# All direct tiles of a block ahead of its products, in a kernel for one step of a streaming encoder

## Chip, core and metric

The kernel runs on one core of a Trainium2 chip. The metric is the device time of one launch in microseconds. A core has five engines with their own instruction streams: TensorE (PE; its weight loads are listed as PEld), VectorE (DVE), ScalarE (ACT), GpSimd (POOL) and SyncE (SP), which here issues nearly all DMAs. They wait for each other through semaphores.

## The reference

One layer with post-norms, on 2048 prompt tokens and 128 sample tokens (8 sequences of 16), width 1024. In short:

```python
qm, km, vm, om, ip, fp, qa, ka, va = split_in(x @ w_in)       # 1024 -> 2824
hm = mlstm_chunkwise(qm, km * 128 ** -0.5, vm, ip + b_igate, log_sigmoid(fp + b_fgate), C0, n0, m0, chunk)
hm = sigmoid(om) * head_norm(hm, g_mlstm_norm)
ha = windowed_attention(rope(qa), rope(ka), va, attn_sinks)    # 8 query heads, 2 key heads
h = layer_norm(ALPHA * x + concat([hm, ha]) @ w_out)
a, g = split(causal_conv3(h @ w_up) + b_conv)                  # 1024 -> 2 * 2816
y = layer_norm(ALPHA * h + (silu(g) * a) @ w_down)
```

Both groups of tokens go through it; beside `y` it returns the states of the memory, the last keys and values and the last rows of the convolution. This case concerns the first line, `x @ w_in`. Its columns fall in two parts: 2560 of them (queries, keys, values, output gate) and 264 (four forget gates, four input gates, and the keys and values of the attention, 128 each).

## The kernel before

All matrices are multiplied in fp32r with three matmuls for one: each operand is split into a high part (a cast on ScalarE, L218 or L566) and a low part (the difference, on VectorE, L219 or L567), and high by high, high by low and low by high are added up in PSUM.

**Stages.** First the input projections in four blocks of four prompt tiles of 128 tokens (`IBLOCKS`; the sample tile belongs to block 0), with the mLSTM and attention work woven in as "chains"; then the output projection in five output blocks (`OBLOCKS`), with the rest of the chains; then the ConvFFN. TensorE's order is the order in which the program is written. The other engines' order is chosen by a scheduler that goes by the order of the program and by when it expects operands to be ready; within one engine, and in SyncE's queue, instructions run in that order.

**Products.** The 2560 columns are done in five groups g (0 to 4) per block. Within a group a matrix product of 2 x 2 sub-blocks is done with seven products instead of eight (a Strassen-like scheme); they are the steps s = 1, 7, 6, 2, 5, 4, 3. Each needs one combination of the token quadrants and one of the weight quadrants. An item `("p", b, g, s)` is one such product: 24 matmuls of 256 columns (L705), and in block 0 for four of the steps 12 more for the sample tile (L715). The results collect in three PSUM banks `ib`, and `i_after` evicts them.

**Direct tiles.** The 264 columns are done directly: an item `("t", b, i, e)` multiplies tile i of block b by the gate weights, 24 matmuls of 264 columns (L731, `i_direct`), into bank `ib[0]` or `ib[2]`. `i_keys` evicts them (ScalarE, L739 and L740), applies the rotary embedding (VectorE, L869 to L872) and stores keys and values (SyncE, L742). The gate weights come in four units of 264 KB, loaded and split anew for every e.

**Tokens.** The tokens of a block are four quadrants of 512 KB, `xr` 1 to 4: quadrants 1 and 3 are the first and second half of the features of tiles 0 and 1, quadrants 2 and 4 those of tiles 2 and 3. `x_load` loads them, and `x_steps` makes the combinations: the split quadrants "1", "2" (quadrant 3), "3" (quadrant 4) and "b12" (quadrant 2), and the sums "t3", "t2", "t1", "t4" with the splits 7, 6, 5 and 4. The direct tiles 0 and 1 need the splits 1 and 2, tiles 2 and 3 need "b12" and 3. A split is kept in a slot of its step, which is free for the next block when the last product of that step is done.

**Order before.** Block 0 begins with its direct tiles 2 and 3, then come the first product and the sample's direct tile. Its direct tiles 0 and 1 come at the end of the block, followed by tiles 2 and 3 of block 1, and so on: at each change of block stand tiles 0 and 1 of the old block and 2 and 3 of the new one, and behind the last block its tiles 0 and 1. `passages` lists after which step of the last group each combination for the next block is made; those of quadrants 1 and 3 (steps 1 and 2) are made behind direct tile 1. For the start, `i_dense` writes out the order of loads and splits; the loads are tokens 2, the gate units, tokens 4, the sample tokens, rotary tables, tokens 1, the weights of group 0, and tokens 3.

**Weaving.** `Chains.weave` adds up a planned cost for each bit of dense work (645 for six matmuls) and lets a chain take its next step when its own due time has passed. While a direct tile of block 1 or later is done, `hold` keeps the chains back. `i_done`, which opens the next block to the chains, is set some items behind the end of a block (`after`).

Of the kernel before, what the change touches and what calls it, by code (L numbers as in the profile page):

```python
# [16 lines left out]
KD = D // P  # L17
# [188 lines left out]
class Prog:  # L206
# [131 lines left out]
    def i_begin(self):  # L338
# [3 lines left out]
        for b in range(nb):  # L342
            if b == 0:
                it += [("t", 0, i, -1) for i in (2, 3)]

                it += [("p", 0, 0, 1), ("t", 0, 4, -1), ("p", 0, 0, 2), ("p", 0, 1, 1), ("p", 0, 0, 7), ("p", 0, 0, 6)]
            else:
                it += [("p", b, 0, s) for s in (1, 7, 6, 2)]
            for g in range(NG):
                if b == 0:  # L350

                    it += [("p", b, g, s) for s in (6, 2)] * (g > 0) + [("p", b, g, 5)]
                    if g + 1 < NG:
                        it += [("p", b, g + 1, 1)] * (g > 0) + [("p", b, g, 4), ("p", b, g, 3), ("p", b, g + 1, 7)]
                    else:
                        it += [("p", b, g, 3), ("p", b, g, 4)]
                elif g + 1 < NG:

                    it += [("p", b, g, s) for s in (6, 7, 2)] * (g > 0)
                    it += [("p", b, g, 5), ("p", b, g + 1, 1), ("p", b, g, 3), ("p", b, g, 4)]  # L360
                else:
                    it += [("p", b, g, s) for s in (6, 7, 5, 2, 3, 4)]
            it += [("t", b, i, b) for i in (0, 1)]
            if b + 1 < nb:
                it += [("t", b + 1, i, b) for i in (2, 3)]
# [169 lines left out]
    def x_load(self, b, *qs):  # L535
        for q in qs:
            self.xr[b, q] = r = self.x_raw(q)
            self.nc.sync.dma_start(r, self.a["xq"][b][(q - 1) // 2, (q - 1) % 2])

    def x_steps(self, b, *steps):  # L540
# [3 lines left out]
        for s in steps:  # L544
# [14 lines left out]
            else:  # L559
# [3 lines left out]
                n = 4 if (b, s) == (0, "b12") else 1  # L563
# [24 lines left out]
    def i_dense(self):  # L588
# [5 lines left out]
        self.x_load(0, 2)  # L594
        for _ in range(3):
            self.next_raw()
        self.x_load(0, 4)
# [3 lines left out]
        self.rope_load(IBLOCKS[0][2], 2)  # L601
        self.rope_load(NPT, 1)
        self.next_split()
        self.x_steps(0, "b12")
        for _ in range(3):
            self.next_split()
        self.x_steps(0, 3)
        self.x_single(1, 2)
        self.x_load(0, 1)
        self.next_raw()  # L610
        self.x_load(0, 3)
        self.x_steps(0, 1)
        self.advance()
        self.x_steps(0, 2, "t3", 7, "t2", 6)
# [4 lines left out]
        passages = [{1: ["load"], 7: ["t3", 7], 6: ["t2", 6], 3: [3, "t4"], 4: ["b12", "t1"]},  # L619
                    {1: ["load"], 6: ["t3"], 7: [7, "t2"], 5: [6], 3: [3, "t4"], 4: ["b12", "t1"]}]  # L620
        sums = 0
        after = None
        for item in self.items:
# [9 lines left out]
            if item[0] == "t":  # L633
# [3 lines left out]
                if b not in self.gates:  # L637
                    self.gates[b] = self.tp.tile([P, 5, 8], F32, name="gates", tag="gates", bufs=2)
                ps = self.bank([P, 512], "pg") if ti == 4 else self.ib[ti % 2 * 2]
                yield from self.i_direct(b, ti, e, ps)  # L640
                self.i_keys(b, ti, ps)
                if ti == 1:
                    if b + 1 < nb:
                        self.x_steps(b + 1, 1, 2)
                    else:
                        self.release(4)
                    after = [6, b + 1]
                elif ti == 3 and b or ti == 4:
                    self.release(4)
                    self.x_steps(b, 4)  # L650
                    if b:
                        self.x_steps(b, 5)
# [14 lines left out]
            if (g, s) == (1, 6):  # L667
                self.rope_load(IBLOCKS[b][0], 2)
            if g == last and b + 1 < nb:
                if s == 7:  # L670
                    self.rope_load(IBLOCKS[b + 1][2], 2)
# [47 lines left out]
    def i_direct(self, b, ti, e, ps):  # L719

        mm = self.nc.tensor.matmul
        for k in range(KD):
# [1473 lines left out]
```

## Time and profile before

| | us |
|---|---|
| median of 3 runs | 2306.43 |
| lowest, highest | 2305.89, 2309.27 |
| the profiled execution's own time | 2306.25 |
| its span in the profile | 2304.5 |
| TensorE busy in the span | 2278.9 (99%) |
| VectorE busy | 1807.4 (78%) |
| ScalarE busy | 1272.4 (55%) |

How to read what follows. Views of the profile name work as line, engine, operation, and out<-in by the program's names. In a timeline a row is: start, duration (both us), engine, line, operation, tiles, sizes, count, and in brackets the idle time of the engine ahead of it with what ended that. In a table by stretch a row is: from:to, length, then for PE, PEld, DVE, ACT and POOL the busy time with the number of instructions in brackets, then the granted clock of TensorE (1 is full), the busy share of the DMA engines, and GB/s; where the table is for one line alone, only the engines of that line stand in it. Matmuls overlap, so the time from one start to the next is what counts, not the duration shown.

### The profile page before, as it was taken

How to read it: one execution, taken by the hardware profiler on the slowest of the kernel's cores; microseconds unless marked ns; L12 is line 12 of the kernel's file. 1: busy time of each engine (PE TensorE's matmuls, PEld its weight loads, DVE VectorE, ACT ScalarE, POOL GpSimd, SP SyncE). 2: the span in 40 equal slices, each digit the busy share in tenths (PEclk: the TensorE clock that was granted, in tenths of full speed). 3: DMA queues.
4: the chain of work that ended last, by engine and by line, in shares of the span. 5: the costliest groups of instructions: out<-in, count | busy, mean ns of one | idle time of the engine just before them, and what ended most of it. 6: DMA issues, size and time to landing. Idle time of an engine off the chain costs nothing.

```text
span 2304.5 us, 39741 instructions
## 1 busy us (share of the span) xinstructions
PE 2278.9 (99%) x14293; PEld 2094.4 (91%) x14293; DVE 1807.4 (78%) x3075; ACT 1272.4 (55%) x2377; POOL 279.4 (12%) x509
## 2 busy tenths in 40 slices
PE   8999999999999999999999999999999999999998
PEld 8999999989877778999999999999999978888876
DVE  8787587787688888998778777678766786895987
ACT  5453476776766656555656555556555544444442
POOL 0001001100011210211112101003111200200200
PEclk9999999999999999999999999999999999999999
DMA  7988999899987757888777888878998786746742
GB/s 267 319 306 297 309 322 342 310 306 341 309 286 239 242 199 277 302 328 300 277 281 272 307 304 310 306 256 289 316 299 260 248 299 213 253 170 223 253 156 83
DMA packets 300165, 632.38 MB, mean 274 GB/s; under 512 B 47868, under 2 KB 141120, under 8 KB 299968
## 3 DMA queue, kind: packets, MB, share of 16 engines
q1 hardware_dynamic: 295296, 616.14, 77.3%
q0 software_dynamic: 3520, 10.56, 1.4%
q10 hardware_dynamic: 1152, 3.15, 0.4%
q8 instruction: 113, 1.85, 0.3%
q14 instruction: 84, 0.69, 0.1%
HBM read 458.11 MB, written 171.64 MB: 273 GB/s over the span
## 4 chain that ended last, share of the span: by engine, by line
PE 81%; DVE 4%; DMA 2%; issue 1%; ACT 1%; POOL 0%; SPq 0%; DVEq 0%; ACTq 0%; POOLq 0%
PE dps L1874 19%; PE fup L1874 19%; PE dps L705 8%; PE fup L2081 6%; PE dps L2081 6%; PE fht L2081 6%; PE dps L223 3%; PE dps L224 2%; PE dps L225 2%; PE ppo L1349 1%; PE psc L1304 1%; PE ppt L1343 1%; PE dps L731 1%; PE fht L1698 1%; PE pscore L1129 1%
## 5 line engine op out<-in xcount | busy, mean ns | idle before, releaser
L1874 PE MATMUL fup<-hh,uw 128*128 128x384 f32 (+1 forms) x1848 | 478.4, 328 | 0.0
L1874 PE MATMUL dps<-hh,uw 128*128 128x384 f32 (+1 forms) x1848 | 478.0, 328 | 0.0
L1874 PEld LDWEIGHTS fup<-hh,uw 128*128 128x128 f32 x1848 | 330.5, 188 | 0.0
L1874 PEld LDWEIGHTS dps<-hh,uw 128*128 128x128 f32 x1848 | 330.3, 188 | 0.0
L1932 DVE SCALAR_TENSOR_TENSOR cc<-u,cw,cc 128x768 f32<-128x768 f32 (+1 forms) x264 | 258.2, 979 | 62.8 <-ACT cc L1930 56.1
L1874 PE MATMUL fup<-hl,uw 128*128 128x384 f32 (+1 forms) x924 | 303.2, 328 | 0.9 <-DVE hl L219 0.9
L1874 PE MATMUL dps<-hl,uw 128*128 128x384 f32 (+1 forms) x924 | 302.8, 328 | 0.0
L705 PE MATMUL dps<-w,oh 128*128 128x256 f32 x1344 | 254.2, 284 | 0.0
L218 ACT CAST uw<-wraw 128x1024 fp32r<-128x1024 f32 x126 | 123.3, 979 | 230.4 <-PE dps L2081 122.4
L219 DVE TENSOR_TENSOR w<-wraw,w 128x1024 fp32r<-128x1024 f32 (+2 forms) x167 | 189.7, 1142 | 66.0 <-ACT w L218 61.9
L218 ACT CAST w<-wraw 128x1024 fp32r<-128x1024 f32 (+2 forms) x167 | 163.0, 984 | 119.0 <-PE dps L705 61.9
L705 PEld LDWEIGHTS dps<-w,oh 128*128 128x128 f32 x1344 | 210.7, 188 | 10.8 <-issue 8.1
L219 DVE TENSOR_TENSOR uw<-wraw,uw 128x1024 fp32r<-128x1024 f32 x126 | 142.5, 1131 | 62.3 <-ACT uw L218 62.2
L705 PE MATMUL dps<-w,ol 128*128 128x256 f32 x672 | 188.1, 280 | 0.0
L1874 PEld LDWEIGHTS fup<-hl,uw 128*128 128x128 f32 x924 | 173.9, 188 | 1.7 <-DVE hl L219 1.5
L2081 PE MATMUL fup<-uw,fu 128*128 128x512 f32 x726 | 174.0, 396 | 1.2 <-ACT fht L2089 1.2
L1874 PEld LDWEIGHTS dps<-hl,uw 128*128 128x128 f32 x924 | 173.8, 188 | 0.0
L705 PE MATMUL dps<-oh,w 128*128 128x256 f32 x896 | 169.6, 285 | 3.6 <-DVE w L219 1.3
L2081 PEld LDWEIGHTS fup<-uw,fu 128*128 128x128 f32 x726 | 136.6, 188 | 34.3 <-ACT fht L2089 1.6
L2081 PE MATMUL dps<-uw,fu 128*128 128x512 f32 x660 | 165.3, 396 | 1.1 <-DVE uw L219 1.1
L1930 ACT ACTIVATE cc<-u,cw 128x768 f32<-128x768 f32 (+1 forms) x132 | 132.0, 1001 | 46.2 <-DVE u L1912 22.2
L2081 PEld LDWEIGHTS dps<-uw,fu 128*128 128x128 f32 x660 | 124.1, 188 | 31.2 <-DVE uw L219 1.5
(318 smaller groups left out, 4590.0 us busy)
## 6 DMA issues: line engine op xcount, KB each, us to landing
uw<-zw SPq DMA_DIRECT2D x176, 512.0 KB, 5.1
zw<-uw SPq DMA_DIRECT2D x88, 512.0 KB, 3.3
w<-zws SPq DMA_DIRECT2D x72, 512.0 KB, 5.8
wv<-wup SPq DMA_DIRECT2D x66, 512.0 KB, 4.4
wraw<-wi SPq DMA_DIRECT2D x65, 512.0 KB, 5.5
wraw<-zt SPq DMA_DIRECT2D x60, 512.0 KB, 4.1
wraw<-wdn SPq DMA_DIRECT2D x45, 512.0 KB, 4.5
wraw<-wo SPq DMA_DIRECT2D x40, 512.0 KB, 4.7
```

Of the source, the lines that this page charges most:

```text
L218: nc.scalar.copy(hi, src)
L219: return nc.vector.tensor_sub(lo, src, hi.bitcast(F32)).ins
L223: mm(out, ah, bh, start=start, stop=False)
L224: mm(out, ah, bl, start=False, stop=False)
L225: mm(out, al, bh, start=False, stop=stop)
L705: mm(o, l, r, start=s in (1, 7) and c == k == i == 0, stop=k == 3 and i == 2, skip_group_check=True)
L731: mm(o, x, w, start=k == i == 0, stop=k == KD - 1 and i == 2, skip_group_check=True)
L1129: self.nc.tensor.matmul(ps[:, h], qk[:, 4 + h], qk[:, h], start=True, stop=True)
L1874: mm(ps, l[:, k], r[:, k], start=s in (1, 7) and k == 0 and i == 0, stop=k == 3 and i == 2, skip_group_check=True)
L1930: S.activation(c[:, v], u[:, 2:2 + n], AF.Identity, bias=w[3], scale=w[2])
L1932: V.scalar_tensor_tensor(c[:, v], u[:, i:i + n], w[i], c[:, v], op0=ALU.mult, op1=ALU.add)
L2081: mm(ps, l[:, k, c], r[:, k], start=s in (1, 4, 7) and u == 0 and k == 0 and i == 0, stop=u == nu - 1 and k == n - 1 and i == 2, skip_grou ...
```

## The change

The direct tiles of a block all come ahead of its products: block 0 begins with its tiles 0 to 3, and at a change of block stand the four tiles of the new block. Behind the last block there are none, and the gate weights are loaded for four sets e instead of five. Tiles 0 and 1 of block 0 are done together by halves: the first four of the eight feature blocks for both, into `ib[0]` and `ib[2]`, then the second four for both, then both evictions. At the start quadrant 1 is loaded first and in two DMAs of two feature blocks each, and split in four pieces (before, quadrant 2 was split in four pieces); quadrant 3 is loaded after the second gate unit; the splits follow in the order 1, 2, "b12", 3. For the other blocks the splits 1 and 2 move into the last group, behind its steps 2 and 5 in block 0 and behind step 2 in the later ones. The rotary tables of both pairs of tiles are loaded at one place. The counter `after` starts behind the last product and counts 8 items instead of 6, so that it ends at the same product of the next block.

```diff
@@ i_begin
-                it += [("t", 0, i, -1) for i in (2, 3)]
+                it += [("t", 0, i, -1) for i in (1, 2, 3)]
...
-            it += [("t", b, i, b) for i in (0, 1)]
             if b + 1 < nb:
-                it += [("t", b + 1, i, b) for i in (2, 3)]
+                it += [("t", b + 1, i, b) for i in range(4)]
@@ x_load
-            self.nc.sync.dma_start(r, self.a["xq"][b][(q - 1) // 2, (q - 1) % 2])
+            x = self.a["xq"][b][(q - 1) // 2, (q - 1) % 2]
+            n = 2 if (b, q) == (0, 1) else 1
+            for i in range(n):
+                k = slice(i * 4 // n, (i + 1) * 4 // n)
+                self.nc.sync.dma_start(r[:, k], x[:, k])
@@ x_steps
-                n = 4 if (b, s) == (0, "b12") else 1
+                n = 4 if (b, s) == (0, 1) else 1
@@ i_dense
         self.next_raw()
-        self.x_load(0, 2)
-        for _ in range(3):
+        self.x_load(0, 1)
+        self.next_raw()
+        self.x_load(0, 3)
+        for _ in range(2):
             self.next_raw()
-        self.x_load(0, 4)
+        self.x_load(0, 2, 4)
...
-        self.rope_load(IBLOCKS[0][2], 2)
+        for i in (0, 2):
+            self.rope_load(IBLOCKS[0][i], 2)
         self.rope_load(NPT, 1)
         self.next_split()
-        self.x_steps(0, "b12")
-        for _ in range(3):
+        self.x_steps(0, 1)
+        self.next_split()
+        self.x_steps(0, 2)
+        for _ in range(2):
             self.next_split()
-        self.x_steps(0, 3)
+        self.x_steps(0, "b12", 3)
         self.x_single(1, 2)
-        self.x_load(0, 1)
         self.next_raw()
-        self.x_load(0, 3)
-        self.x_steps(0, 1)
         self.advance()
-        self.x_steps(0, 2, "t3", 7, "t2", 6)
+        self.x_steps(0, "t3", 7, "t2", 6)
...
-        passages = [{1: ["load"], 7: ["t3", 7], 6: ["t2", 6], 3: [3, "t4"], 4: ["b12", "t1"]},
-                    {1: ["load"], 6: ["t3"], 7: [7, "t2"], 5: [6], 3: [3, "t4"], 4: ["b12", "t1"]}]
+        passages = [{1: ["load"], 7: ["t3", 7], 6: ["t2", 6], 2: [1], 5: [2], 3: [3, "t4"], 4: ["b12", "t1"]},
+                    {1: ["load"], 6: ["t3"], 7: [7, "t2"], 5: [6], 2: [1, 2], 3: [3, "t4"], 4: ["b12", "t1"]}]
...
+                if b == 0 and ti == 1:
+                    for h in range(2):
+                        for i in range(2):
+                            yield from self.i_direct(b, i, e, self.ib[i * 2], (h,))
+                    self.i_keys(b, 0, self.ib[0])
+                    self.i_keys(b, 1, self.ib[2])
+                    self.advance()
+                    continue
...
-                if ti == 1:
-                    if b + 1 < nb:
-                        self.x_steps(b + 1, 1, 2)
-                    else:
-                        self.release(4)
-                    after = [6, b + 1]
-                elif ti == 3 and b or ti == 4:
+                if ti == 3 and b or ti == 4:
...
-            if (g, s) == (1, 6):
-                self.rope_load(IBLOCKS[b][0], 2)
+            if (g, s) == (last, 4):
+                after = [8, b + 1]
...
-                    self.rope_load(IBLOCKS[b + 1][2], 2)
+                    for i in (0, 2):
+                        self.rope_load(IBLOCKS[b + 1][i], 2)
@@ i_direct
-    def i_direct(self, b, ti, e, ps):
+    def i_direct(self, b, ti, e, ps, halves=(0, 1)):
...
-        for k in range(KD):
+        for k in [4 * h + i for h in halves for i in range(4)]:
```

## The prediction

> **What bounds the kernel now.** I read the head of the page first, then who TensorE waited for between 100 and 700 us, then the stretches of the start.
>
> ```profile
> span 2304.5 us, 39741 instructions
> PE 2278.9 (99%) x14293; PEld 2094.4 (91%) x14293; DVE 1807.4 (78%) x3075; ACT 1272.4 (55%) x2377; POOL 279.4 (12%) x509
> ...
> PE ppt L1518 <- POOL v L1094: 2.9, 1, 2.9
> PE pnum L1212 <- issue: 1.9, 2, 1.4
> PE dps L705 <- ACT mr L1154: 0.8, 1, 0.8
> PE ppo L1349 <- ACT pth L1344: 0.6, 1, 0.6
> ```
>
> TensorE is busy 99% of the span: 25.6 us are left idle, and a change that moves matmuls without removing any can win only idle time and time at a lower clock. In the second view (waits by engine and line: total, times, longest) no direct tile (L731) stands: the changes of block at 155, 292, 453 and 620 us cost TensorE nothing today, so nothing is to be won there. What is left for this change is the start. The next two views are stretches: of the direct tiles alone, of the products (L705) alone, and of all engines.
>
> ```profile
> 5.99:18.26 12.27, 9.89 (x48) 8.72 (x47) 0.72 1.03 408
> 155.07:166.74 11.67, 11.67 (x96) 11.62 (x96) 1.00 0.93 307
> 620.34:626.28 5.94, 5.94 (x48) 5.89 (x48) 1.00 0.82 290
> ...
> 38.16:45.63 7.47, 5.17 (x28) 4.56 (x26) 0.77 0.85 292
> 45.63:48.52 2.89, 2.89 (x24) 2.86 (x24) 1.00 0.98 398
> ...
> 9.00:12.00 3.00, 1.20 (x3) 0.89 (x4) 2.06 (x3) 2.18 (x3) 0.00 (x0) 0.70 1.04 408
> 12.00:17.00 5.00, 5.00 (x24) 5.00 (x24) 3.76 (x9) 2.78 (x8) 0.00 (x0) 0.50 1.03 421
> 41.00:45.00 4.00, 3.94 (x21) 3.73 (x19) 4.00 (x6) 1.03 (x3) 0.00 (x0) 0.59 0.79 229
> ```
>
> Four direct tiles take 11.67 us when nothing is late (0.122 us a matmul, two tiles 5.84). At the start two tiles take 12.27: 6.4 us are lost there, and the granted clock (the number before the DMA share) is 0.70 and then 0.50 behind the waits. The product of step 6 (38.16 to 45.63) takes 7.47 us where the next takes 2.89: 4.6 us more. These two places are most of what can be had.
>
> ```profile
> 8.01 0.39 PE L731 MATMUL dps<-w,oh 128*128 128x264 f32 x1 [0.46 <-DVE w L219]
> 10.36 0.81 PE L731 MATMUL dps<-w,oh 128*128 128x264 f32 x2 [1.47 <-ACT oh L566]
> 11.62 0.59 PE L731 MATMUL dps<-w,ol 128*128 128x264 f32 x1 [0.45 <-DVE ol L567]
> 26.11 0.39 PE L705 MATMUL dps<-ol,w 128*128 128x256 f32 x1 [0.42 <-DVE ol L567]
> 35.66 0.50 PE L705 MATMUL dps<-oh,w 128*128 128x256 f32 x2 [0.48 <-DVE w L219]
> 39.21 0.38 PE L705 MATMUL dps<-oh,w 128*128 128x256 f32 x1 [0.78 <-ACT w L218]
> 40.55 0.53 PE L705 MATMUL dps<-oh,w 128*128 128x256 f32 x2 [0.84 <-DVE w L219]
> 45.63 0.38 PE L705 MATMUL dps<-oh,w 128*128 128x256 f32 x1 [0.69 <-ACT zev L772]
> ...
> 4.13 0.41 ACT L566 CAST oh<-xr 128x256 fp32r<-128x256 f32 x1 [2.11 <-DMA xr<-xq]
> 9.26 1.04 ACT L566 CAST oh<-xr 128x1024 fp32r<-128x1024 f32 x1 [0.61 <-DMA xr<-xq]
> ...
> 4.56:18.26 13.70, 11.32 (x52) 9.77 (x52) 10.83 (x22) 8.72 (x18) 0.00 (x0) 0.75 1.01 391
> 18.26:40.43 22.17, 19.78 (x160) 18.81 (x158) 21.46 (x29) 12.16 (x17) 0.00 (x0) 1.00 0.58 200
> ```
>
> These are TensorE's and ScalarE's rows in order of time (what was waited for in brackets) and two stretches of all engines. The wait of 1.47 us is for the second quadrant of tokens, which lands at 9.2 us (ScalarE's row). From 26 to 41 us every wait ends with VectorE or with the cast in front of it, and VectorE is busy 21.46 of 22.17 us there. So the start has two limits: DMA until about 10 us, VectorE until 40.5.
>
> **The change, part by part.**
>
> *Matmuls moved.* Tiles 0 and 1 of each block go from behind its products to in front of them: 48 matmuls, 5.84 us, more at the start, and the last block's pair (5.94 us at 620.34) is gone. Sum 0. The four gate-weight units of the last block (264 KB each, a cast and a subtraction each) go too; nothing waited for them, 0.
>
> *Order of loading.* Before: quadrant 2, four gate units, quadrant 4; the first half tile needs 512+528 KB, all 48 matmuls 2080 KB. After: quadrant 1 in two halves, two gate units, quadrant 3, the other units, then 2 and 4. The 2080 KB were in at 9.2 us, the first 512 at 4.1: 307 KB a us (estimate from the two ScalarE rows), later 421 GB/s. In the new order that gives unit 0 at 5.0, unit 1 at 5.8, quadrant 3 at 7.5, the last unit at 9.2, quadrant 2 at 10.5, quadrant 4 at 11.7. The next rows price the work on them (VectorE by form up to 45 us: busy, mean ns; SyncE's issues).
>
> ```profile
> L567 DVE TENSOR_TENSOR ol<-xr,oh 128x1024 fp32r<-128x1024 f32 x5 | 6.1, 1223 | 0.9 <-ACT oh L566 0.9
> L219 DVE TENSOR_TENSOR w<-wraw,w 128x528 fp32r<-128x528 f32 x4 | 2.8, 708 | 0.7 <-ACT w L218 0.6
> L872 DVE TENSOR_TENSOR zev<-zev,rb 128x128 f32<-128x128 f32 x3 | 0.9, 289 | 0.0
> L871 DVE TENSOR_TENSOR zev<-zev,ropet 128x128 f32<-128x128 f32 x3 | 0.9, 288 | 0.0
> L869 DVE TENSOR_TENSOR rb<-zev,ropet 128x64 f32<-128x64 f32 x3 | 0.7, 225 | 1.2 <-ACT zev L739 1.1
> L870 DVE TENSOR_TENSOR rb<-zev,ropet 128x64 f32<-128x64 f32 x3 | 0.7, 219 | 0.0
> ...
> 39.28 3.49 DVE L219 TENSOR_TENSOR w<-wraw,w 128x1024 fp32r<-128x1024 f32 x3
> ...
> 0.74 0.39 SPq L538 DMA_DIRECT2D xr<-xq  x1
> 15.70 8.47 SPq L742 DMA_DIRECT2D zkv<-zev  x2
> 24.70 1.76 SPq L456 DMA_DIRECT2D wraw<-wi  x3
> ```
>
> *TensorE at the start, after.* It starts at 5.99 as now, the warm-up ends there. The first halves of both tiles are 24 matmuls, 2.9 us, with some 0.8 us of waits for the low parts of units 0 and 1 (now 0.46): done at 9.7. The second halves need quadrant 3's low part: 7.5 + 1.04 (cast) + 1.23 = 9.8, then unit 2's: + 0.71 = 10.5. A wait of 0.8 us, where there were 1.47 and 0.45. Done at 13.4. Tiles 2 and 3 follow without a wait (quadrant 4's low part at 11.7 + 2.3 = 14.0, needed at 14.9) and end at 19.2. Now this point is 18.26 with two tiles: 5.84 - 0.94 = 4.9 us won there.
>
> *VectorE then.* It keeps that gain or takes it back. Its work up to the low part of step 6 (the first of three at 39.28, so 40.5) is the same splits and sums, plus the rotary of tiles 0 and 1: 0.289 + 0.288 + 0.225 + 0.219 = 1.02 us each, 2.0 in all. Its idle time up to there is 2.87 + 0.71 = 3.6 us. I take it that 1.3 us of that is filled, as all four quadrants have landed by 11.7 and VectorE has work from 14 us on without a break; the other 2.3 lie ahead of 14 us, where it waits for landings in both orders. So the low part comes at 40.5 + 2.0 - 1.3 = 41.2. Bounds: 2.0 later if nothing is filled, 1.6 earlier if all is. TensorE would reach that product at 19.2 + (38.16 - 18.26) less the waits of 0.42 and 0.48 = 38.2, so VectorE still sets the pace; some waits of the start come back in front of steps 7 and 6, and I let the lower clock there stand. Step 6 ends 0.7 us later than now with 5.84 us more behind it: 5.1 us won, between 3.8 and 7.4. The wait of 0.69 behind it is for the eviction of the same bank and stays.
>
> *Queues.* SyncE issues one load more for the halves and one rotary table more (0.4 us each); its queue runs ahead of the landings, 0. It also stores the keys of four tiles, not two, each behind a rotary: those two stores held it from 15.70 to 24.17 now, and the next group's weights went out at 24.70. Held some 4 us longer they would go out near 29; the group that they belong to has its other products behind the one that starts at 45.63: 0. ScalarE gets two more evictions of keys into its idle time. The direct tiles of the first block share two banks; tile 2 must wait for tile 0's eviction, which has the 1.46 us of tile 1's second half: 0, at worst 0.3.
>
> *Changes of block.* The splits of quadrants 1 and 3 for the next block (two casts of 1.04, two subtractions of 1.22) move from between the direct tiles to the last group, since their slots are free after its steps 1 and 2. They must be done when step 4 ends, two products later (5.7 us). VectorE is full there at the third change:
>
> ```profile
> 445.00:450.00 5.00, 5.00 (x48) 4.73 (x48) 4.72 (x18) 4.46 (x12) 0.59 (x1) 1.00 0.74 248
> 450.00:455.00 5.00, 5.00 (x46) 5.00 (x45) 4.93 (x7) 5.00 (x15) 0.57 (x1) 1.00 0.89 302
> ...
> 285.00:290.00 5.00, 5.00 (x45) 5.00 (x44) 2.75 (x7) 2.53 (x4) 1.29 (x2) 1.00 0.83 259
> ...
> 873.95 0.61 ACT L897 CAST oh<-xraw 128x512 fp32r<-128x512 f32 x1
> ```
>
> 9.65 of 10 us, while ahead of the second change (285 to 290) almost half is free. What waits behind those splits is the next block's quadrants 4 and 2, due two direct tiles (5.84 us) later. I take 0, with -1.5 to +3 as bounds: the gain if the waits of 1.9 and 0.8 us above shrink because VectorE is freer behind the change of block.
>
> *The end of the projections.* The chains of attention and memory pause during direct tiles; the last pair falls away, so they enter the output blocks up to 5.9 us behind in that order. What hangs on them last is the final quarter of tokens for the last output block: its cast is at 873.95 us (last row above), and TensorE, which waits for no such cast now, needs it some microseconds later (not shown how many). I take 0, with 2 as the far end (half the shift not covered; an estimate).
>
> **Sum.** 2306.25 (the profiled execution, 1.75 us outside its span) - 5.1 = 2301.2. That execution is 0.2 us under the median of 2306.43.
>
> [...]
>
> **Rivals.**
> 1. *The clock holds in front of step 6.* It was 0.59 for 21 matmuls in 4 us, 0.19 us each against 2.89/24 = 0.12: 1.5 us. For it: TensorE's matmuls arrive more evenly. Against it: VectorE is as late as now. 2301.2 - 1.5 = 2299.7.
> 2. *VectorE hides the gain.* None of its idle time is filled (3.8 us) and a wait of the kind seen now at 26 us (0.42) and another of 0.8 in front of a bank turn up: 2304. For it: it has 2 us more work ahead of the same deadline.
> 3. *The last group becomes late: slower.* If, at 453 us, the moved splits end behind step 4, TensorE stands at the first direct tile and falls to half clock. Price by the start: a wait of about 2.4 us and 4.0 more for the lower clock (6.4 lost less 2.4), 6.4 a place. One place eats the 5.1; two make 2314. It decides from a delay of about 3 us of that subtraction on. For it: 9.65 of 10 us busy. Against: the splits are spread over two products, and only one of three places is so full.
> 4. *The halves do nothing*, because the loads are issued in another order than written: the start waits as now, VectorE still limits: 2302 to 2303, inside the second rival's range.
>
> **How the numbers follow.** Forecast 0.48 (own range 2299.8 to 2302.8), rival 1 0.14, rivals 2 and 4 together 0.23, rival 3 0.15. The predicted time is the likeliest's. The range 2297.5 to 2307.5 takes in rivals 1 and 2 and the bounds of the changes of block, and leaves out most of rival 3. A change under 0.2% (4.6 us) can hardly be told from none: below 2301.8 lie rival 1 and three quarters of the forecast, 0.51; above 2311.0 most of rival 3, 0.14; the rest 0.35.
>
> **What would show it.** Right: four direct tiles from about 6 to 19 us, no wait over 1 us before 14 us; step 6's low part at about 41; no L731 wait at the three changes of block; since each change of block has four direct tiles as before, these start about 0.7 us later than now (155.07), and the gain shows only where the output blocks start: about 621, not 626.3. Wrong: a clock of 0.5 between 9 and 17 us again; a wait at a first direct tile for a low part (L567); waits in the output blocks, where there is none now.

## The result and the profile after

The changed kernel takes 2312.3 us (median of 18 runs, 2307.65 to 2317.83) against 2307.15 for the kernel before (18 runs, 2303.51 to 2313.78): a ratio of 1.0025, 95% interval 1.0017 to 1.0032. It is slower by 5 to 6 us (4 to 7 by the interval), where a gain to 2301.2 was forecast. The profiled execution took 2312.08 us.

The head of the page after:

```profile
span 2310.3 us, 39709 instructions
PE 2279.2 (99%) x14293; PEld 2093.3 (91%) x14293; DVE 1807.8 (78%) x3071; ACT 1270.5 (55%) x2373; POOL 280.0 (12%) x509
```

Who TensorE waited for in it between 100 and 640 us (total, times, longest):

```profile
PE ppt L1351 <- ACT pth L1352: 4.1, 2, 2.7
PE ppt L1526 <- POOL v L1102: 2.9, 1, 2.9
PE dps L713 <- ACT mr L1162: 2.1, 1, 2.1
PE dps L713 <- ACT zev L772: 2.1, 1, 2.1
PE pnum L1220 <- DVE dt L1141: 2.0, 1, 2.0
```

Before, the list began with 2.9, 1.9, 0.8 and 0.6. The 2.9 for GpSimd is the same wait; five new ones of 1.4 to 2.7 us have come (four rows), all behind ScalarE or VectorE in the work of attention and memory (L1351, L1220) or in the products (L713, which was L705), and none at a direct tile (L739, which was L731). The start and the changes of block, by stretch, in the columns explained above:

```profile
12.00:17.00 5.00, 5.00 (x44) 5.00 (x43) 3.77 (x6) 2.89 (x8) 0.00 (x0) 1.00 1.04 413
41.00:45.00 4.00, 2.92 (x23) 2.72 (x24) 4.00 (x9) 2.19 (x3) 0.00 (x0) 1.00 0.97 316
...
154.41:166.10 11.69, 11.69 (x99) 11.69 (x98) 9.54 (x19) 5.88 (x12) 0.00 (x0) 1.00 0.87 300
292.80:304.50 11.70, 11.70 (x99) 11.70 (x98) 11.34 (x21) 7.41 (x16) 0.00 (x0) 1.00 0.93 308
459.70:471.40 11.70, 11.70 (x99) 11.70 (x98) 11.36 (x23) 9.82 (x23) 0.00 (x0) 1.00 0.85 288
```

The start does more than was forecast: the clock is 1.00 where it was 0.50 (12 to 17 us, which the forecast had counted on) and 0.59 (41 to 45 us, which it had not). At the changes of block TensorE has no gap. So the loss lies between them. TensorE's order is the same in both kernels from block 1 to the end of the projections, so the start of each matmul can be set against the start of the same one before. Where the changed kernel has done two more direct tiles by then, their 5.84 us are taken off. The difference (negative is ahead), worked out from the traces:

| at us of the trace before | 57 | 253 | 262 | 320 | 345 | 410 | 505 | 570 | 900 |
|---|---|---|---|---|---|---|---|---|---|
| after | -6.6 | -6.5 | -4.9 | -5.5 | -1.5 | +0.9 | -0.6 | +5.2 | +5.6 |

6.6 us are won at the start and kept to 253 us. Then, up to 570 us, 11.7 are lost: 1.6 at 254, 4.0 and 2.4 between 320 and 410, 5.8 between 505 and 570, less gains of 0.6 and 1.5 between. Two stretches there, for TensorE alone (busy time with the number of matmuls, granted clock, DMA share, GB/s), first of the kernel before and then of the changed one:

```profile
320.00:345.00 25.00, 23.09 (x187) 1.00 1.01 343
500.00:530.00 30.00, 29.46 (x247) 1.00 0.99 336
```

```profile
320.00:345.00 25.00, 20.77 (x156) 0.93 0.91 307
500.00:530.00 30.00, 27.05 (x204) 0.94 0.88 285
```

31 and 43 matmuls fewer in the same time: waits, and a lower clock behind them. Following one of them back gives the cause. These are VectorE's, ScalarE's and TensorE's rows of the changed kernel in order of time (in brackets the idle time and what ended it):

```profile
323.45 0.69 DVE L859 TENSOR_TENSOR txy<-txy 128x512 f32<-128x512 f32 x1 [2.21 <-DMA txy<-wdn]
324.06 0.15 DVE L1319 SCALAR_TENSOR_TENSOR amx<-amx,nsink 128x4 f32<-128x4 f32 x1
326.95 0.69 DVE L860 TENSOR_TENSOR txy<-txy 128x512 f32<-128x512 f32 x1 [2.74 <-DMA txy<-wdn]
...
324.31 0.41 ACT L1324 ACTIVATE sc<-sc,amx 128x129 f32<-128x129 f32 x1 [4.88 <-DVE amx L1319]
331.77 0.17 ACT L1162 ACTIVATE mr<-pnum 128x2 f32<-128x2 f32 x1 [4.38 <-DVE bst L1159]
...
327.04 0.39 PE L713 MATMUL dps<-oh,w 128*128 128x256 f32 x1 [2.10 <-ACT zev L772]
333.44 0.38 PE L713 MATMUL dps<-oh,w 128*128 128x256 f32 x1 [2.13 <-ACT mr L1162]
```

L859 to L862 are the sums of the down weights. The ConvFFN at the end also works with sums of weight quadrants, and `d_sums` makes them in blocks 2 and 3, ahead of their use: two loads of 512 KB (L853, L854) into a tile `txy`, which lies in the slots of `xr` 1 and 3, four subtractions on VectorE, two stores. Nobody needs them for a long time. But VectorE works in its order. It stands 2.21 and 2.74 us for the loads, and behind it stand the last step of the softmax's maximum (L1319; the maxima it works on were done at 321.24 us, and it runs at 324.06, behind L859), for which ScalarE waits 4.88 us, and the statistics of the norm (L1159), for which it waits 4.38; ScalarE's own evictions (L772) stand behind these, and TensorE waits 2.10 for such an eviction and then 2.13, by its row for L1162, which had itself waited those 4.38. Before, at this place the sums came behind that work and stood for nothing:

```profile
323.51 0.46 DVE L1151 BATCH_NORM_STATS2 bst<-pnum 128x6 f32<-128x128 f32 x2
332.13 0.69 DVE L851 TENSOR_TENSOR txy<-txy 128x512 f32<-128x512 f32 x1
332.85 0.69 DVE L852 TENSOR_TENSOR txy<-txy 128x512 f32<-128x512 f32 x1
```

Over 300 to 570 us VectorE's waits for `txy` are, before and then after (total, times, longest):

```profile
DVE txy L852 <- DMA txy<-wdn: 4.6, 3, 3.6
DVE txy L851 <- DMA zqk<-zev: 4.2, 1, 4.2
DVE txy L851 <- DMA txy<-wdn: 2.9, 1, 2.9
```

```profile
DVE txy L859 <- DMA txy<-wdn: 13.4, 5, 3.5
DVE txy L860 <- DMA txy<-wdn: 5.4, 3, 2.7
```

11.7 us became 18.8. (One row of before, 4.2, is put down to another DMA than the load.) The sum of these waits is not the price: it grew by 7.1 and TensorE lost 11.7, while two other kernels below (the start alone, and the kernel before without the logs) have waits of 12.0 and 12.9 and TensorE loses 0.2 us or less over the same stretch. What counts is what stands behind each. A load takes 5.5 us from issue to landing before and 6.4 after (medians of the DMA view over the same stretch, 512 KB each):

```profile
txy<-wdn SPq DMA_DIRECT2D x15, 512.0 KB, 5.5
```

```profile
txy<-wdn SPq DMA_DIRECT2D x16, 512.0 KB, 6.4
```

### The profile page after: what moved, and what is told of

Its sections match the earlier page's. It is cut to its first block, busy times and chain, and to the rows that moved or that the text cites. A ratio compares the mean times of both kernels' runs of the same rounds, so it can differ in the third digit from the quotient of the medians.

```text
span 2310.3 us, 39709 instructions
## 1 busy us (share of the span) xinstructions
PE 2279.2 (99%) x14293; PEld 2093.3 (91%) x14293; DVE 1807.8 (78%) x3071; ACT 1270.5 (55%) x2373; POOL 280.0 (12%) x509
## 4 chain that ended last, share of the span: by engine, by line
PE 81%; DVE 4%; DMA 2%; issue 1%; ACT 0%; POOL 0%; SPq 0%; DVEq 0%; ACTq 0%; POOLq 0%
PE dps L1882 20%; PE fup L1882 19%; PE dps L713 8%; PE fup L2089 6%; PE dps L2089 6%; PE fht L2089 6%; PE dps L223 3%; PE dps L225 2%; PE dps L224 2%; PE ppo L1357 1%; PE ppt L1351 1%; PE psc L1312 1%; DMA txy<-wdn 1%; PE fht L1706 1%; DVE w L219 1%
## 5 line engine op out<-in xcount | busy, mean ns | idle before, releaser
L713 PE MATMUL dps<-w,oh 128*128 128x256 f32 x1344 | 255.3, 285 | 0.0
L713 PEld LDWEIGHTS dps<-w,oh 128*128 128x128 f32 x1344 | 211.5, 189 | 10.9 <-issue 8.1
L713 PE MATMUL dps<-w,ol 128*128 128x256 f32 x672 | 188.2, 280 | 0.0
L713 PE MATMUL dps<-oh,w 128*128 128x256 f32 x896 | 170.2, 285 | 7.1 <-DVE w L219 2.2
L713 PEld LDWEIGHTS dps<-oh,w 128*128 128x128 f32 x896 | 141.6, 190 | 13.9 <-issue 4.5
```

Of the source, the lines that this page charges most:

```text
L713: mm(o, l, r, start=s in (1, 7) and c == k == i == 0, stop=k == 3 and i == 2, skip_group_check=True)
```

## The experiments

Three theories were set against each other. **Theory 1**: VectorE stands at the sums for their late loads, and the work behind them carries that to TensorE. **Theory 2**: the splits moved into the last group crowd VectorE there (the mechanism of the forecast's third rival). **Theory 3**: any shift of the start makes the scheduler plan the later blocks anew, by chance for the worse. The table below has TensorE's lead (negative) or lag against the kernel before, formed as above, for the kernels that follow.

| | 57 | 253 | 262 | 320 | 345 | 410 | 505 | 570 | 900 |
|---|---|---|---|---|---|---|---|---|---|
| after | -6.6 | -6.5 | -4.9 | -5.5 | -1.5 | +0.9 | -0.6 | +5.2 | +5.6 |
| start alone | -6.3 | -2.2 | -2.2 | -2.2 | -2.3 | -2.3 | -3.8 | -2.2 | -2.4 |
| later part alone | -0.7 | -0.7 | +0.7 | +0.1 | +2.8 | +5.9 | +4.7 | +9.1 | +9.9 |
| after, earlier loads | -6.3 | -6.2 | -6.2 | -6.4 | -6.2 | -4.6 | -6.2 | -7.3 | -7.5 |
| before, earlier loads | -2.4 | -2.4 | -1.1 | -1.1 | +4.5 | +4.5 | +3.0 | +2.2 | +2.8 |
| before, no sums | +0.4 | +0.4 | +0.4 | -0.2 | -0.3 | +0.3 | -1.2 | -2.3 | +0.5 |
| after, no sums | -6.5 | -6.4 | -6.4 | -7.1 | -8.8 | -3.4 | -4.9 | -6.0 | -6.3 |
| after, sums on GpSimd | -6.4 | -6.3 | -4.8 | -4.2 | -3.0 | +4.5 | +4.5 | +7.9 | +17.4 |
| after, logs late | -6.6 | -6.6 | -5.3 | -5.9 | 0.0 | +0.4 | -1.1 | +3.7 | +3.4 |
| after, logs late, splits twice | -6.3 | -6.3 | -6.3 | -7.0 | -3.6 | -3.6 | -2.3 | +3.9 | +3.6 |
| earlier loads, no halves | -2.8 | -2.8 | -1.3 | -1.0 | -0.7 | -0.6 | -1.3 | -2.3 | -2.4 |

Each row is one execution, and the start differs by execution: six kernels have the start of the kernel before, the same instructions in the same order, and at 57 us they stand at 0 (before itself), -0.7, -2.4, +0.4 and, not in the table, 0.0 and -2.5 (the sums earlier, the logs left out); the eight with the whole new start stand at -5.8 to -6.6. So the kernel before is one of the slower of its six, and the new start is worth about 5.5 us, the difference of the two means, rather than 6.6.

### The start alone

Block 0 as changed, the changes of block as before (against the changed kernel):

```diff
             if b + 1 < nb:
-                it += [("t", b + 1, i, b) for i in range(4)]
+                it += [("t", b + 1, i, b) for i in (2, 3)]
...
+            if b:
+                it += [("t", b, i, b) for i in (0, 1)]
...
-        passages = [{1: ["load"], 7: ["t3", 7], 6: ["t2", 6], 2: [1], 5: [2], 3: [3, "t4"], 4: ["b12", "t1"]},
+        passages = [{1: ["load"], 7: ["t3", 7], 6: ["t2", 6], 3: [3, "t4"], 4: ["b12", "t1", 1, 2]},
...
```

> Only the start of the change: block 0 takes tiles 0 and 1 first, by halves, with the new order of loads; the changes of block at 292, 453 and 620 us stay as before. The trace of the changed kernel is 0.8 us ahead at 57 us with 5.84 us of matmuls more behind it (6.6 us won), and loses 11.8 us between 254 and 559 us. If the loss comes with the moved splits and tiles of the later blocks (theory 1: VectorE stands at loads for the sums of the down weights, which the new order of the later blocks brings forward; theory 2: the moved splits crowd the last group), this kernel keeps the 6.6 us: 2300 to 2302 against 2307 of before. If any shift at the start re-plans the later blocks for the worse (theory 3), it loses part of that: 2304 to 2313, with VectorE waits on txy like those of the changed kernel.

2307.03 us against 2307.46, ratio 0.9998 (0.9989 to 1.0006). The 2300 to 2302 of theories 1 and 2 is missed, and by its number the run lies in theory 3's range. The table shows why: the start wins its 6.3, loses 4.1 at the first change of block, and the later blocks then lose nothing more. The 4.1 are this kernel's own: with tiles 0 and 1 of block 0 gone from there, the change has two tiles and not four, and the first of them comes for a split that had 5.84 us more before:

```profile
157.26 0.39 PE L748 MATMUL dps<-w,ol 128*128 128x264 f32 x1 [2.14 <-DVE ol L572]
```

The rest of the 4.1 is mostly the clock behind it, 0.82 over these 5 us of TensorE and 0.84 over the next 5:

```profile
155.00:160.00 5.00, 2.86 (x16) 0.82 0.88 296
```

Against theory 3 speaks the stretch from 253 to 410 us: the start moved by 2 us, and the lead stays at 2.2 to 2.3. One shift cannot refute a theory of chance; the next run, which has the loss without the shift, and the two that keep a shift of over 6 us without the loss (the changed kernel with earlier loads, and without the sums) leave it nothing to explain.

### The later part alone

The start and block 0 as before, the four tiles in front and the moved splits from block 1 on (against the kernel before):

```diff
-            it += [("t", b, i, b) for i in (0, 1)]
+            if b == 0:
+                it += [("t", b, i, b) for i in (0, 1)]
             if b + 1 < nb:
-                it += [("t", b + 1, i, b) for i in (2, 3)]
+                it += [("t", b + 1, i, b) for i in ((2, 3, 0, 1) if b == 0 else range(4))]
...
-                    {1: ["load"], 6: ["t3"], 7: [7, "t2"], 5: [6], 3: [3, "t4"], 4: ["b12", "t1"]}]
+                    {1: ["load"], 6: ["t3"], 7: [7, "t2"], 5: [6], 2: [1, 2], 3: [3, "t4"], 4: ["b12", "t1"]}]
...
```

> Only the later part of the change: start and block 0 as before, at the first change of block tiles 0 and 1 of block 0 and then tiles 2, 3, 0, 1 of block 1, at the others four tiles of the new block, splits 1 and 2 in the last group of blocks 1 and 2. Theories 1 and 2: slower than before by some 8 to 12 us (2315 to 2319), with the losses between 320 and 560 us. Theory 3: about as before, 2305 to 2310.

2317.87 us, ratio 1.0053 (1.0038 to 1.0068). The later part costs 10 to 12 us by itself (the trace, the medians), at the same places as in the changed kernel. So the two halves of the change are separate: a start that wins 5.5 to 6.6, a later part that costs 10 to 12.

### The loads of the sums earlier

The loads of a pair are issued one group ahead, into slots 2 and 4 or 1 and 3 in turn; the sums stay where they are. Once in the changed kernel and once in the kernel before:

```diff
-                if s in steps:
+                if s == steps[0]:
+                    for n in ([0] if g == 0 else []) + ([g + 1] if g + 1 < last else []):
+                        self.d_fetch(sums + n - g, (1, 3) if n % 2 else (2, 4))
+                elif s in steps:
+                    self.txy = self.fetched[sums]
                     self.d_sums(sums, steps.index(s))
...
```

> The changed kernel with the operands of the down-weight sums loaded one group earlier, into two pairs of buffers (quadrants 2 and 4, then 1 and 3) instead of one; the same sums at the same places. Theory 1: VectorE no longer waits for txy, TensorE's waits at 327, 333, 395, 522 and 559 us go, 2300 to 2303. Theory 2: the waits stay, since the splits are where they were: 2310 to 2314. Theory 3 says nothing of this.

> The kernel before with the same earlier loads. It waits 11.7 us on VectorE for txy too, at places where TensorE hardly shows it (waits of 0.5 to 1.4 us at 320, 328, 500, 548). Theory 1: a little faster than before, 2303 to 2307. If the earlier loads help by themselves and have nothing to do with the change, it gains as much as the changed kernel does with them: 2296 to 2300.

The changed kernel takes 2300.98 us with it, ratio 0.9974 (0.9964 to 0.9984): 11 us less than without, and the fastest of the kernels here that leave nothing out. VectorE's waits for `txy` between 300 and 570 us fall from 18.8 to 5.1 us:

```profile
DVE txy L870 <- DMA txy<-wdn: 3.6, 2, 2.6
DVE txy L869 <- DMA txy<-wdn: 1.5, 1, 1.5
```

The kernel before gains nothing: 2309.29, ratio 1.0009 (1.0000 to 1.0018), above the 2303 to 2307 that theory 1 gave. Its trace is still the clearest picture of theory 1, by the longest of five waits that are left (VectorE, ScalarE, TensorE):

```profile
325.56 0.69 DVE L861 TENSOR_TENSOR txy<-txy 128x512 f32<-128x512 f32 x1 [4.00 <-DMA txy<-wdn]
330.32 0.17 ACT L1164 ACTIVATE mr<-pnum 128x2 f32<-128x2 f32 x1 [5.73 <-DVE bst L1161]
331.99 0.58 PE L710 MATMUL dps<-oh,w 128*128 128x256 f32 x1 [5.65 <-ACT mr L1164]
```

One wait of 4.00 us on VectorE, 5.73 on ScalarE behind it, 5.65 on TensorE behind that: the 5.6 us of the table between 320 and 345.

### The sums left out

The four subtractions of each pair are taken out of both kernels (loads and stores stay; the down products then get plain weights for their sums):

```diff
-            V.tensor_sub(x[:, l], x[:, r], x[:, l])
-            V.tensor_sub(x[:, r], y[:, r], x[:, r])
-            V.tensor_sub(y[:, r], y[:, r], x[:, l])
-            V.tensor_sub(y[:, l], y[:, l], y[:, r])
```

> The kernel before without the four subtractions of each pair of down weights: the loads and stores stay, the sums are left out (so the down products get the plain weights). 11 pairs of 4 x 0.68 us of VectorE go, and every wait for their loads. Theory 1: before lost little to them, 2304 to 2307. Theories 2 and 3: the same, this run is the measure for the next.

> The changed kernel without the four subtractions of each pair: nothing is left for VectorE to stand at. Theory 1: the start's 6.6 us stay won, so 5 to 7.5 us under the kernel before without them: 2298 to 2301. Theory 2: the change still costs 5 us against it, as with the sums: 2309 to 2312. Theory 3: between the two, 2302 to 2308.

2306.19 us for the kernel before (ratio to it 1.0000, 0.9991 to 1.0010) and 2300.67 for the changed one (0.9969, 0.9958 to 0.9980). This settles the main question. With the sums the change costs 5.2 us, without them it wins 5.5; the loads and stores are still there, the moved splits too. Theory 2 is refuted by it, and so is the guess that the change at its core could not pay. Not every step of the table is the sums: without them the changed kernel still gains 1.6 us from 320 to 345 and loses 5.4 from 345 to 410, behind two waits for a ScalarE instruction (3.0 us together) that the changed kernel does not have.

### The sums moved in the program

The sums one or two products later in the changed kernel (their stores one to three), and one product earlier in the kernel before:

```diff
-                steps = (6, 2, 5) if g == last - 1 else (6, 5, 3)
+                steps = (6, 5, 4) if g == last - 1 else (6, 3, 4)
```

```diff
-                steps = (6, 2, 5) if g == last - 1 else (6, 5, 3)
+                steps = (6, 7, 5) if g == last - 1 else (6, 2, 3)
```

> The changed kernel with nothing moved but the sums of the down weights: VectorE's four subtractions of a pair stand one product later in the program (two in a block's first group), their loads stay where they are. Theory 1 (VectorE stands at sums whose loads have not landed): in the changed kernel it stood 18.8 us at eight such instructions; one product is 4 to 6 us, longer than each of the waits of 1.3 to 3.5 us, so they go, PE's waits at 327, 333, 395 and 522 us with them, and the time is 2300 to 2304, near the 2301 of the kernel with earlier loads. Theory 2 (the moved splits crowd the last group): the sums do not matter, 2311 to 2313. Theory 3 (any shift plans the later blocks anew, for the better or the worse by chance): 2306 to 2313, with waits at other places.

> The kernel before with nothing moved but the sums of the down weights, one product earlier in the program, so that their loads are late for them. Theory 1: VectorE stands at them some 2 to 4 us each in the six groups of two blocks, half of the groups pass it on to PE, 2312 to 2320, with PE waits behind ScalarE and VectorE between 315 and 560 us. Theory 2: the start of the kernel and its splits are untouched, 2306 to 2308. Theory 3: 2304 to 2312.

2312.68 us (ratio 1.0026, 1.0016 to 1.0037) and 2307.12 (0.9998, 0.9988 to 1.0007): both expectations of theory 1 missed, because the edits did nothing to VectorE's order: its instructions up to 640 us come in the same sequence as without them. In the first, the second pair's first sum stands at 324.76 us with a wait of 2.8 as if nothing had been moved; in the second, it stays at 332.15. The place of the sums in VectorE's order does not follow their place in the program within a product or two; as the scheduler goes by when it expects operands, the likely reason is that it puts them where it expects their loads. These runs tell nothing for or against the theories, and they rule out the simplest cure.

### Sums on GpSimd

```diff
-            V.tensor_sub(x[:, l], x[:, r], x[:, l])
+            nc.gpsimd.tensor_sub(x[:, l], x[:, r], x[:, l])
```

(and the other three likewise, in the changed kernel)

> The changed kernel with the sums of the down weights on GpSimd, everything else as it is: the loads are as late as before, but it is GpSimd that stands for them and not VectorE. GpSimd was busy for 25.7 of the 270 us between 290 and 560 us, and a product of 128x512 took it 1.3 us against VectorE's 0.68, so a pair takes some 5.2 us there. Theory 1 (it is VectorE's standing that reaches PE): no wait for txy is left on VectorE, PE's waits at 327, 333, 395 and 522 us go, 2298 to 2303; what could spoil it is work of the chains on GpSimd behind a standing sum (the powers of the norms, the copies of the sink), which would give PE waits of a few us and up to 2306. If the late loads cost the time in some other way (their traffic, their place in SP's list): 2310 to 2314.

2323.49 us, ratio 1.0061 (1.0041 to 1.0081), above every range that was given. GpSimd's waits for `txy` between 300 and 570 us:

```profile
POOL txy L859 <- DMA txy<-wdn: 66.1, 8, 14.4
POOL txy L860 <- DMA txy<-wdn: 17.3, 6, 4.5
```

From 320 to 345 us, where the changed kernel lost 4.0, this one loses 1.2, with no wait for `txy` on VectorE: it is VectorE's standing that costs there, not the lateness of the loads as such. From 345 to 410 it loses 7.5 where the changed kernel lost 2.4, and what ends its longest wait there, 3.6 us, is VectorE again (L1141), with no sum on it. GpSimd's order holds chain work too, a subtraction takes it 1.5 to 1.8 us on average, and the total is worse by 11 us, most of it in the output blocks, where another three pairs are made (from +7.9 at 570 to +17.4 at 900). An engine that is 12% busy is no safe place for an instruction that waits.

### What put the sums ahead of their loads

There are two suspects, the logs and the splits. The logs of a block's gates (14 small instructions of VectorE, 2.3 to 2.6 us) can start a block earlier once all four tiles come in front: before they ran at 307 and 468 us, after at 169 and 382. First they alone were held back, then also the splits 1 and 2 were made a second time where they lay before; the third kernel takes work away from the kernel before (for the blocks after the first the logs are left out, only the lesser of gate and nought is taken).

```diff
         e, d, s, s2 = w
         p = d
         V = nc.vector
+        if b + 1 in self.gates:
+            V.scalar_tensor_tensor(x[:, :1], self.gates[b + 1][:, 1:2, 0:4], 0.0, x[:, :1], op0=ALU.mult, op1=ALU.add)
```

```diff
                 self.i_keys(b, ti, ps)
+                if b and ti == 1:
+                    for s, q in ((1, 1), (2, 3)):
+                        (h, l), x = self.hx[b, s], self.xr[b, q]
+                        nc.scalar.copy(h, x)
+                        nc.vector.tensor_sub(l, x, h.bitcast(F32))
```

```diff
         V = nc.vector
+        if b:
+            V.tensor_scalar_min(x, x, 0.0)
+            return g
```

> The changed kernel with the logs of a block's gates (14 small instructions of VectorE, 2.3 to 2.6 us) held back until the second direct tile of the next block has its gates, which is where they lay before: one more instruction adds nought times those gates. In the changed kernel these logs ran at 169, 382 to 412 and 533 us, before at 307, 468 and 629. Theory 1 with this as its trigger (the logs come a block earlier, VectorE's list is shorter behind 305 us, the sums move ahead of their loads): the logs of blocks 1 and 2 return to some 305 and 470 us, the second pair of sums to some 330 us, PE's waits at 327 and 333 us (4.7 us with the half clock) go, and some of those at 395 and 522 us: 2301 to 2307. Theory 1 with another trigger, or theory 2: 2310 to 2314, with waits for txy as in the changed kernel.

> The changed kernel with the logs of the gates late as in the run before, and with the splits of the first two quarters made a second time where they lay before (between the second and the third direct tile of a change of block: two copies of ScalarE of 1.0 us and two subtractions of VectorE of 1.2 us, same values), so that VectorE's list behind a change of block is again as long as before. If the length of that list is what puts the sums in front of their loads: the second pair of sums goes back behind the softmax work at some 330 us, the PE waits at 328 and 335 us go, 2303 to 2309 (with some us for the second splits themselves). If it is not: 2310 to 2316, with waits for txy of 2 to 4 us at some 325 us as in the two runs.

> The kernel before with less work on VectorE: for the blocks after the first the logs of the gates are left out (the gates go on as the lesser of the gate and nought), some 14 small instructions, 2.3 us, at 307, 468 and 629 us. Theory 1 with this trigger: the sums move ahead on VectorE's list, it stands for their loads, and the kernel gets slower by doing less: 2308 to 2313, with txy waits between 320 and 330 us and PE waits of over 1 us behind them. Without this trigger: 2305 to 2307.

2311.34 us (ratio 1.0025, 1.0012 to 1.0037), 2311.1 (1.0013, 1.0002 to 1.0025) and 2306.93 (0.9999, 0.9989 to 1.0009). The logs went back to 300 and 467 us as wanted, and the second pair still stood, 4.1 and 2.9 us at 325 and 328: the earlier logs are not what it needs. But with the logs left out of the kernel before, the first sum of that pair did move ahead, from 332.13 to 319.55 us, and stood for its load:

```profile
319.55 0.69 DVE L851 TENSOR_TENSOR txy<-txy 128x512 f32<-128x512 f32 x1 [1.04 <-DMA txy<-wdn]
```

The other three stayed behind the softmax work (327.90 us and later), and TensorE lost 0.1 us from 320 to 345. So taking work off VectorE can bring a sum forward, and costs time only where something urgent stands behind it. With the splits repeated, half of the pair went back:

```profile
324.31 0.69 DVE L864 TENSOR_TENSOR txy<-txy 128x512 f32<-128x512 f32 x1 [3.16 <-DMA txy<-wdn]
332.94 0.68 DVE L865 TENSOR_TENSOR txy<-txy 128x512 f32<-128x512 f32 x1
```

and the loss from 320 to 410 us fell from 6.4 to 3.4, while that behind 505 us stayed; the total missed the 2303 to 2309 hoped for. So the splits that the change moved away from the change of block are part of what reorders VectorE's list, and not all. What else does stays open.

### The halves undone

With the earlier loads kept, so that nothing else disturbs: tile 0 whole and then tile 1 whole, quadrant 1 loaded and split in one piece.

```diff
-            n = 2 if (b, q) == (0, 1) else 1
+            n = 1
...
-                n = 4 if (b, s) == (0, 1) else 1
+                n = 1
...
-                    for h in range(2):
-                        for i in range(2):
-                            yield from self.i_direct(b, i, e, self.ib[i * 2], (h,))
+                    for i in range(2):
+                        yield from self.i_direct(b, i, e, self.ib[i * 2])
```

> The kernel with the change and the earlier loads, but the first block's first two tiles one after the other and whole, with the first load and its splits whole as well. Taken as the forecast took the halves: 1 to 2 us more at the start, 2302 to 2303.5 against 2301, the difference to be read at 57 us of the trace. If the halves do nothing: 2301. If the change owes them most of its start: 2304 or more.

2303.87 us, ratio 0.9987 (0.9977 to 0.9997); with the halves it was 0.9974. At 57 us the lead is 2.8 and not 6.3, and the medians are 2.9 apart: the halves, with the first load and its splits in pieces, are worth 2.9 to 3.5 of the start's 6.3 us, more than the 1 to 2 expected. The waits come back in the first tiles (three of 0.8 to 1.0; the clock from 12 to 17 us is 0.66), and inside step 6 the wait for its low part is 1.82 where it was 1.00 with the halves:

```profile
7.24 0.39 PE L743 MATMUL dps<-w,oh 128*128 128x264 f32 x1 [0.96 <-DVE w L219]
9.62 0.39 PE L743 MATMUL dps<-w,oh 128*128 128x264 f32 x1 [0.78 <-ACT w L218]
10.97 0.39 PE L743 MATMUL dps<-w,oh 128*128 128x264 f32 x1 [0.96 <-DVE w L219]
44.14 0.50 PE L717 MATMUL dps<-oh,w 128*128 128x256 f32 x2 [1.82 <-DVE w L219]
```

## Why the prediction was wrong, step by step

**The start: right in mechanism, 5.1 us forecast, 6.6 measured at 57 us.** The four direct tiles ran from 6.0 to 20.1 us (19.2 forecast) with no wait over 0.4; the 0.9 cost nothing, as VectorE sets the pace behind them, as said: step 6's low part came at 41.4 (41.2 forecast). The 1.5 are the first rival, which was given 0.14: in step 6 the clock held, 1.00 from 41 to 45 us where it was 0.59, behind a wait of 0.79 us where it had been 0.84. That is in part luck of the execution that was taken as the measure. The kernel before with earlier loads has the same start, and its clock held there too, behind a wait of 0.82:

```profile
41.00:45.00 4.00, 3.31 (x29) 3.12 (x28) 3.96 (x6) 1.36 (x3) 0.00 (x0) 1.00 0.69 195
```

In two of the six executions with the old start the clock held there, in four it was 0.59 to 0.66; with the new order of tiles it held in all nine. Between the means of the two groups the start wins 5.5 us, near the forecast. The second rival (VectorE hides the gain) did not come, and neither did the fourth: the halves do something.

**Queues and tile 2's bank: 0, right.** No row of TensorE between 11.38 and 33.23 us has a wait.

**Changes of block: 0, with -1.5 to +3 as bounds: this is the step that failed.** The direct tiles there do have no waits, at 453 us (now 459.7) neither, so the third rival's place and mechanism were wrong, though it alone had the right sign. The step looked at what waits for the moved splits and for nothing behind the change. It took VectorE being "freer behind the change of block" for a possible gain. The runs show a loss: with the splits gone from there, VectorE's list is reordered (the splits are part of the reason, the rest is open), the sums of the down weights come ahead of loads that take 6.4 us in the median, and VectorE stands 18.8 us for them, with work behind it that TensorE needs. Price: 11.7 us in the trace, with the 1.6 at 254, whose cause is open (11.3 by the earlier loads; 10.7 by leaving the sums out, from +5.2 to -5.5). The output blocks began at 631.4 us, not at 621. The waits for `txy` could be read in the trace of before (11.7 us over 300 to 570): a place where a list already stood for late loads, with nothing behind it for which TensorE waited long.

**The end of the projections: 0, with 2 as the far end: right.** From 570 to 900 us the changed kernel loses 0.4.

**The sum and the range.** -6.5 + 11.7 + 0.4 is +5.6, against the spans' 5.8. No term of the sum and no rival held a loss of this kind, so the range ended at 2307.5. Without the sums in the way, or with their loads early, the changed kernel takes 2300.7 and 2301.0, where 2301.2 was forecast. That these meet so closely is in part luck: the forecast subtracted 5.1 from one execution of 2306.25, while the median of the kernel before is 2307.15, and the gains are 5.5 (without the sums in both kernels) and about 6 (earlier loads, by the ratio).

## What to carry to other kernels

When a change moves work on an engine that a scheduler orders, look for every instruction of that engine that waits for a DMA and that nobody needs soon: its place is a guess of when the load lands, and if it slips ahead, what stands behind it waits with it (here VectorE stood 18.8 us). Give such loads more lead (another buffer, a group earlier) before judging the change, since it may be the better kernel: here the same edit was 5 us slower without that and about 6 us faster with it. Moving such an instruction by a product or two in the program, or to an idler engine, did not help. And before a part of a trace is taken as the measure of a gain, see how much that part differs between executions: here the same start differed by up to 2.9 us.

## What the runs showed of the hardware

The clock does not follow the length of a gap alone. The same wait of 2.85 us for GpSimd lies at 254 us in both kernels; the stretches behind it, before and after:

```profile
253.00:258.00 5.00, 4.04 (x36) 1.00 0.96 327
```

```profile
253.00:258.00 5.00, 4.71 (x27) 0.66 0.60 203
```

This is the 1.6 us at 254 in the table. Of the fifteen kernels' profiles it fell there in seven, two with earlier loads among them, and held in eight (in the table six lose 1.3 to 1.6 us from 253 to 262, the others nothing); one profile of each cannot say whether that belongs to a kernel or to an execution. At the start the same program gave both: in step 6, behind waits of 0.82 to 0.84 us, four executions of the old start went on at a clock of 0.59 to 0.66 and two at 1.00. The forecast put the clock of 0.70 and then 0.50 in the first tiles behind the waits there, which were 0.46, 1.47 and 0.45 us; behind the first of them the matmuls still came 0.12 us apart (8.24 to 8.60 us), and the 0.22 us of the half clock are seen only behind the third (from 12.00 us on).

VectorE kept its order while it waited: L1319 ran at 324.06 us, behind the sum, with its maxima done at 321.24. The three rows of 4.00, 5.73 and 5.65 us show what that can cost.
